# Weight tiles split into two parts by casting and accumulating DMAs from DRAM, with no raw copy in SBUF

## The chip, the cores and the metric

The kernel runs on one core of one Trainium2 chip. The metric is device time in microseconds (us) of one execution. Lower is better. The core has five engines with instruction queues of their own, each worked off in order: PE (matrix products; PEld is its weight load), DVE (VectorE), ACT (ScalarE), POOL (GpSimd) and SP (SyncE). SP and POOL both issue DMAs here: SP's go through the hardware queue q1, POOL's through the software queue q0. Both are carried out by the same 16 DMA engines.

## The reference

One decoder block over 512 tokens (plus 16 meta tokens put in front) of width 1024, all in float32:

```
h = concat(meta, x)                                   # (528, 1024)
proj = rmsnorm(h, g_mix) @ w_in                       # z 1024 | xbc 1536 | dt 16 | u 1024 columns
y_ssd = ssd(silu(conv(xbc)), dt, z)                   # Mamba-2 heads: 16 heads, state 128
y_s5  = glu(gelu(s5(u)) @ w_glu + b_glu)              # 64 groups, state 64; w_glu (1024, 2048)
h = h + concat(y_ssd, y_s5) @ w_out                   # w_out (2048, 1024)
h = h + square(relu(rmsnorm(h, g_mlp) @ w_up)) @ w_down   # w_up (1024, 4096), w_down (4096, 1024)
out = rmsnorm(h, g_final)[16:]
```

## The kernel before

A float32 product is made from three products of operands in the rounded format `fp32r`: each operand is split into a high part `hi` (the value rounded) and a low part `lo` (the rest, rounded), and PE adds hi x hi, hi x lo and lo x hi into one PSUM bank (`mm_cols` for weights on the stationary side, `rows_product` for weights on the moving side). So every weight has to be loaded and split before PE can use it.

Weights come in tiles of 128 partitions x 1024 values (512 KB). There are 92 of them that go through the functions which the change touches, in this order of use: 8 column tiles of `w_in` for u (first projection), 8 for z, 12 for xbc, 16 of `w_glu`, 16 row tiles of `w_out`, 32 column tiles of `w_up`. A column tile is 8 x 128 pieces of 128 values (512 bytes) in DRAM, a row tile 2 x 128 pieces of 512 values (2 KB). The weights of `w_down` (32 tiles, called `quad` and `quads`) are loaded and split by other functions.

`load_weight` has SP load a tile into `raw` (two buffers). `split_weight` then makes `whi` and `wlo` (three buffers each) in one of two ways. With `lo_engine` V (45 tiles: one of u, 12 of `w_out`, 32 of `w_up`) ACT casts `raw` to `whi` and DVE subtracts. Otherwise (47 tiles: 7 of u, z, xbc, `w_glu` and 4 of `w_out`) ACT writes -raw, rounded, to `wlo`, a DMA issued by POOL adds `raw` to it from SBUF, and ACT casts `raw` to `whi`.

The stages overlap. While PE works on z and xbc, it, DVE and ACT also work off the blocks of the S5 scan (`s5_block`, with tiles `px`, `py`, `pb`, `pk`). While it works on the GLU (`pv`, `pg`), the chunks of the SSD run, which need large broadcasts from DRAM (`ab`, `erep`) and a masking step on POOL (the affine select). In the MLP four quarters follow each other: 8 tiles of `w_up` (`pm`), then a down product (`acc`, `acct`) in which two tiles of the next quarter are already used. At the start POOL also computes the powers of the first norm (`rstd`).

The order of the instructions on each engine is set by a scheduler that plays the program through with its own times before it is built. `tc.high_priority(offset=3000)` moves the loads and the splits forward in it as far as their buffers allow; within an engine's queue nothing overtakes on the chip. PSUM has three banks (`mm`) for the products with column tiles.

Of the kernel before, what the change touches and what calls it, by code (L numbers as in the profile page):

```python
# [18 lines left out]
P = 128  # L19
# [5 lines left out]
KD = DM // P  # L25
# [4 lines left out]
O_U = 2576  # L30
# [8 lines left out]
AHEAD = 3000  # L39
# [14 lines left out]
def hybrid_block_kernel(ctx, tc, x, meta_tokens, g_mix, w_in, conv_w, conv_b, dt_bias, a_log, d_ssd,  # L54
                        g_ssd, lam_re, lam_im, log_step, b_re, b_im, c_re, c_im, d_s5, w_glu, b_glu,
                        g_s5, w_out, g_mlp, w_up, w_down, g_final, out, dbg=None):
    nc = tc.nc
    V, A, G, T = nc.vector, nc.scalar, nc.gpsimd, nc.tensor
    dma = nc.sync.dma_start
# [8 lines left out]
    wp = ctx.enter_context(tc.tile_pool(name="wp", bufs=2))  # L68
# [30 lines left out]

    def load_weight(src, a, b, ahead=AHEAD):
        with (tc.high_priority(offset=ahead) if ahead else nullcontext()):
            raw = wp.tile([P, a, b], F32, tag="raw", name="raw", bufs=2)
            dma(out=raw, in_=src)
        return raw

    def split_weight(raw, lo_engine=None, ahead=AHEAD, room=None):
        with (tc.high_priority(offset=ahead) if ahead else nullcontext()):
            if room is None:  # L110
                hi = wp.tile(list(raw.shape), F32R, tag="hi", name="whi", bufs=3)
                lo = wp.tile(list(raw.shape), F32R, tag="lo", name="wlo", bufs=3)
            else:
                hi, lo = room("whi", list(raw.shape)), room("wlo", list(raw.shape))
            if lo_engine is V:
                A.copy(hi, raw)  # L116
                V.tensor_tensor(out=lo, in0=raw, in1=hi.bitcast(F32), op=ALU.subtract)  # L117
            else:

                A.mul(lo, raw, -1.0)  # L120
                G.dma_start(out=lo.bitcast(F32), in_=raw, accum_op=ALU.add)  # L121
                A.copy(hi, raw)  # L122
        return hi, lo

    def load_cols(w, c0, n=P, ahead=AHEAD):
        return load_weight(w[:, c0:c0 + n].rearrange("(k p) c -> p k c", p=P), KD, n, ahead)

    def w_cols(w, c0, n=P, lo_engine=None):
        return split_weight(load_cols(w, c0, n), lo_engine)

    def w_rows(w, k0, c0, lo_engine=None, room=None):
        return split_weight(load_weight(w[k0 * P:(k0 + 2) * P, c0:c0 + 512].rearrange("(k p) c -> p k c", p=P),
                                        2, 512), lo_engine, room=room)

    def mm_cols(ps_out, w, x, m, tok):
        steps = [(k, a, b) for k in range(KD) for a, b in ((0, 0), (0, 1), (1, 0))]
# [55 lines left out]
    first_raw = {}  # L192
# [49 lines left out]
    uw, uts = {}, {}  # L242

    def u_split(f):
        raw = first_raw[f] if f in first_raw else load_cols(w_in[0], O_U + f * P)
        uw[f] = split_weight(raw, V if f == 2 else G, 0 if f < 3 else AHEAD)
        uts[f] = s5.tile([P, TS5, NC5], F32, tag="ut", name="ut", bufs=2)

    def u_half(f, i):
# [180 lines left out]
    for part, (x0, x1, op) in enumerate(((bRt, bIt, ALU.subtract), (bIt, bRt, ALU.add))):  # L430
# [3 lines left out]
                        in1=tb2.rearrange("p (b j) h -> p b j h", b=8), op=op)  # L434
# [236 lines left out]
    for f in range(8):  # L671
        w = w_cols(w_in[0], f * P)
# [15 lines left out]
    for f in order:  # L688
        w = w_cols(w_in[0], O_XBC + f * P)
# [4 lines left out]
    for n, f in enumerate(order):  # L694
        raw = xbc_tile(f)
# [27 lines left out]
    for ch in range(NCH):  # L723
        n = NM if ch == 0 else P
# [14 lines left out]
        if ch > 0:  # L739
            lt = slice((ch - 1) * P, ch * P)  # L740
            erep = sd.tile([P, KD, P], F32, tag="erep", name="erep", bufs=1)
            for q in range(2):
                dma2(out=erep[64 * q:64 * q + 64],
                     in_=eD.rearrange("(r q) l -> q r l", q=2)[q, :, lt].partition_broadcast(64))
# [14 lines left out]
            for h in range(2):  # L759
# [8 lines left out]
                for r in range(4):  # L768
# [6 lines left out]
                                op=ALU.mult)  # L775
# [38 lines left out]
    token_rstd(s1, pq1[:, 0:4])  # L814


    def rows_product(lhs, w, rows0, n_slab, c0, lo_engine, finish, room=None):
        acc = [None if room else bank("acc") for _ in range(4)]

        def mms(sl, wt, t):  # L820
            for k in range(2):
                for n, (a, b) in enumerate(((0, 0), (1, 0), (0, 1))):
                    T.matmul(acc[t], lhsT=lhs[2 * sl + k][a][:, t * P:(t + 1) * P], rhs=wt[b][:, k],  # L823
                             start=(sl == 0 and k == 0 and n == 0), stop=(sl == n_slab - 1 and k == 1 and n == 2))


        tail = 1 if room is None else n_slab
        for sl in range(n_slab - tail):
            wt = w_rows(w, rows0 + 2 * sl, c0, lo_engine)
            for t in range(4):  # L830
                mms(sl, wt, t)
        last = [(sl, w_rows(w, rows0 + 2 * sl, c0, lo_engine, room if sl else None))
                for sl in range(n_slab - tail, n_slab)]
# [36 lines left out]
    y5hi = slot("y5hi", [P, KD, SEQ], F32R)  # L870
    y5lo = slot("y5lo", [P, KD, SEQ], F32R)
# [31 lines left out]
    s2 = mid.tile([P, 4], F32, tag="s5_s", name="s5_s", bufs=1)  # L903
    token_rstd(s2, pq2[:, 0:4])
    for c0 in (0, 512):
        rows_product([(y5hi[:, k], y5lo[:, k]) for k in range(KD)], w_out[0], 8, 4, c0, V, add_scaled(s2))
    yhi = slot2("yhi", [P, KD, SEQ], F32R)
    ylo = slot2("ylo", [P, KD, SEQ], F32R)
    for f in range(8):
        A.activation(out=yhi[:, f], in_=xc[:, f, NM:L], func=AF.Copy, scale=col("gssd", f))  # L910
        V.scalar_tensor_tensor(out=ylo[:, f], in0=xc[:, f, NM:L], scalar=col("gssd", f),
                               in1=yhi[:, f].bitcast(F32), op0=ALU.mult, op1=ALU.subtract)
# [17 lines left out]
        transpose_split(xs[:, t], P, hhi, hlo, t * P)  # L930

    ylist = [(yhi[:, k], ylo[:, k]) for k in range(KD)]
    rows_product(ylist, w_out[0], 0, 4, 0, G, mix_first)
    spare = iter(("S", "xdt", "xde", "erep", "ab", "ab"))

    def spare_room(name, shape):
        tag = next(spare)
        return sd.tile(shape, F32R, tag=tag, name=name, bufs=2 if tag == "ab" else 1)

    rows_product(ylist, w_out[0], 0, 4, 512, V, mix_second, room=spare_room)  # L940


    sd_ctx.__exit__(None, None, None)
# [211 lines left out]
```

## Time and profile before

| | |
|---|---|
| three runs | 854.35, 854.48, 850.58 us |
| median | 854.35 us |
| profiled execution, its own time | 849.42 us |
| its span in the profile | 847.7 us |
| mean granted TensorE clock | 0.976 |
| instructions in the span | 11641 |
| bytes on q1 (SP's DMAs) | 90.89 MB, 37.1% of the 16 engines' span |
| bytes on q0 (POOL's DMAs) | 24.64 MB, 15.6% |

The profile is one execution. Its page gives busy times of the engines, the span in 40 slices with a digit for the busy tenths, the DMA queues, and a chain of waits: the work that ended last, followed back from the end. Other views list groups of instructions (how many, busy time, mean of one in ns, then the idle time of the engine before them and what ended it), a tile's instructions (min/median/max in ns, then first and last start in us), and a stretch of the span. A matmul's recorded time overlaps with that of the next one, so PE's pace is read from the distance of starts, or from a piece of the chain and its count.

### The profile page before, as it was taken

To read this page: it belongs to the slowest core of one execution; us is meant where nothing else is said; L and a number is where in the kernel's file an instruction comes from. 1 tells how busy PE (TensorE), PEld (TensorE's weight loads), DVE (VectorE), ACT (ScalarE), POOL (GpSimd) and SP (SyncE) were. 2 spreads that over 40 slices of the span, in tenths; PEclk is the share of its full clock that TensorE was granted. 3 is DMA by queue.
4 is the path that set the end of the run, shared out by engine and by line. 5 is a ranking of instruction groups with operands and counts; after the bars stand their busy time and mean duration, and the time that the engine had idled before them with its cause. 6 is when DMAs were issued, how large, how long until landed. Compare 5 with 4: busy or idle time off the path is not lost.

```text
span 847.7 us, 11641 instructions
## 1 busy us (share of the span) xinstructions
PE 793.3 (94%) x4351; PEld 668.9 (79%) x4351; DVE 585.5 (69%) x961; ACT 453.8 (54%) x714; POOL 66.9 (8%) x115
## 2 busy tenths in 40 slices
PE   5998699999996789988999999999999999999996
PEld 4898588999994667776888888888888888888874
DVE  6873688899973585561631567688848884887396
ACT  7575678798664457474313344354334524443264
POOL 5101010101010122111001010000000000000001
PEclk9999899999998899999999999999999999999999
DMA  9887666677657568778426636434133422331002
GB/s 221 188 201 188 149 154 146 168 156 171 153 143 169 162 136 186 164 208 212 144 98 149 176 97 224 125 99 150 51 98 100 150 71 83 118 127 49 1 2 99
DMA packets 144865, 116.28 MB, mean 137 GB/s; under 512 B 22092, under 2 KB 122616, under 8 KB 144808
## 3 DMA queue, kind: packets, MB, share of 16 engines
q1 hardware_dynamic: 138040, 90.89, 37.1%
q0 software_dynamic: 6768, 24.64, 15.6%
q8 instruction: 34, 0.56, 0.3%
q14 instruction: 23, 0.19, 0.1%
HBM read 83.93 MB, written 6.95 MB: 107 GB/s over the span
## 4 chain that ended last, share of the span: by engine, by line
PE 66%; DMA 17%; issue 4%; ACT 4%; SPq 4%; DVE 3%; POOL 0%; POOLq 0%; ACTq 0%; DVEq 0%
PE pm L138 21%; PE acc L1066 15%; PE acc L823 8%; DMA wlo<-raw 6%; PE pxb L138 4%; PE pz L138 4%; DMA raw<-in_w_in_dram 4%; DMA ab<-aD 3%; PE acct L823 3%; PE acct L1066 3%; DMA yf<-Yd 2%; PE pg L138 1%; PE px L561 1%; PE pv L138 1%; ACT wlo L120 1%
## 5 line engine op out<-in xcount | busy, mean ns | idle before, releaser
L117 DVE TENSOR_TENSOR wlo<-raw,whi 128x1024 fp32r<-128x1024 f32 x45 | 55.0, 1222 | 78.4 <-ACT whi L116 78.3
L138 PE MATMUL pm<-hhi,wlo 128*128 128x512 f32 (+1 forms) x272 | 103.6, 381 | 0.0
L138 PE MATMUL pm<-hlo,whi 128*128 128x512 f32 (+1 forms) x272 | 103.5, 381 | 0.0
L138 PE MATMUL pm<-hhi,whi 128*128 128x512 f32 (+1 forms) x272 | 103.0, 381 | 0.0
L116 ACT CAST whi<-raw 128x1024 fp32r<-128x1024 f32 x45 | 47.2, 1049 | 101.5 <-PE pm L138 60.3
L122 ACT CAST whi<-raw 128x1024 fp32r<-128x1024 f32 x47 | 49.0, 1043 | 57.8 <-PE acc L823 15.3
L1066 PE MATMUL acc<-bh,al 128*128 128x512 f32 x192 | 75.1, 391 | 0.1
L1066 PE MATMUL acc<-bl,ah 128*128 128x512 f32 x192 | 75.0, 391 | 0.0
L1066 PE MATMUL acc<-bh,ah 128*128 128x512 f32 x192 | 69.5, 392 | 1.4 <-ACT ah L970 1.4
L121 POOL DMA_DIRECT2D wlo<-raw x47 | 40.2, 856 | 313.4 <-ACT wlo L120 148.0
L970 ACT CAST bh<-quad 128x1024 fp32r<-128x1024 f32 x32 | 33.7, 1053 | 49.4 <-PE acc L1066 42.3
L138 PEld LDWEIGHTS pm<-hlo,whi 128*128 128x128 f32 x272 | 51.1, 188 | 10.9
L138 PEld LDWEIGHTS pm<-hhi,whi 128*128 128x128 f32 x272 | 51.0, 188 | 10.8
L138 PEld LDWEIGHTS pm<-hhi,wlo 128*128 128x128 f32 x272 | 51.0, 188 | 10.4
L138 PE MATMUL pxb<-xhi,whi 128*128 128x264 f32 x192 | 56.3, 293 | 0.0
L138 PE MATMUL pxb<-xlo,whi 128*128 128x264 f32 x192 | 56.2, 293 | 0.0
L138 PE MATMUL pxb<-xhi,wlo 128*128 128x264 f32 x192 | 56.0, 292 | 0.0
L120 ACT ACTIVATE wlo<-raw 128x1024 fp32r<-128x1024 f32 x47 | 49.6, 1054 | 8.6 <-DMA raw<-in_w_glu_dram 8.1
L965 DVE TENSOR_TENSOR bl<-quad,bh 128x1024 fp32r<-128x1024 f32 x32 | 39.1, 1221 | 18.6 <-ACT bh L970 18.6
L970 ACT CAST bh<-quads 128x1024 fp32r<-128x1024 f32 x24 | 25.2, 1049 | 40.8 <-PE acc L1066 26.7
L1066 PEld LDWEIGHTS acc<-bh,ah 128*128 128x128 f32 x192 | 35.9, 188 | 9.7 <-ACT ah L970 2.1
L1066 PEld LDWEIGHTS acc<-bh,al 128*128 128x128 f32 x192 | 36.0, 188 | 8.3 <-DVE al L965 0.5
(374 smaller groups left out, 2062.6 us busy)
## 6 DMA issues: line engine op xcount, KB each, us to landing
wlo<-raw POOLq DMA_DIRECT2D x47, 512.0 KB, 5.1
raw<-in_w_up_dram SPq DMA_DIRECT2D x32, 512.0 KB, 4.0
raw<-in_w_in_dram SPq DMA_DIRECT2D x28, 512.0 KB, 4.0
raw<-in_w_glu_dram SPq DMA_DIRECT2D x16, 512.0 KB, 4.4
raw<-in_w_out_dram SPq DMA_DIRECT2D x16, 512.0 KB, 3.2
quad<-in_w_down_dram SPq DMA_DIRECT2D x16, 512.0 KB
quads<-in_w_down_dram SPq DMA_DIRECT2D x16, 512.0 KB, 6.0
ab<-aD SPq DMA_DIRECT2D x8, 512.0 KB, 6.5
```

The lines of the kernel that those rows point to most:

```text
L116: A.copy(hi, raw)
L117: V.tensor_tensor(out=lo, in0=raw, in1=hi.bitcast(F32), op=ALU.subtract)
L120: A.mul(lo, raw, -1.0)
L121: G.dma_start(out=lo.bitcast(F32), in_=raw, accum_op=ALU.add)
L122: A.copy(hi, raw)
L138: T.matmul(ps_out, lhsT=w[a][:, k, 0:m], rhs=x[b][:, k, tok], start=(n == 0), stop=(n == len(steps) - 1))
L561: T.matmul(p[:, j * NC5:(j + 1) * NC5], lhsT=w[:, 2 * hf + j], rhs=ub[:, 2 * hf + j])
L823: T.matmul(acc[t], lhsT=lhs[2 * sl + k][a][:, t * P:(t + 1) * P], rhs=wt[b][:, k], start=(sl == 0 and k == 0 and n == 0), stop=(sl == n_sl ...
L965: V.tensor_tensor(out=out, in0=a, in1=b, op=ALU.subtract)
L970: A.copy(hi, src)
L1066: T.matmul(banks[bk][s], lhsT=as_[g][x][:, j, s * P:(s + 1) * P], rhs=bs[g][y][:, j], start=(first and g == 0 and j == 0 and i == 0), stop ...
```

## The change

All 92 tiles are treated alike. `whi` is written by a DMA from POOL that reads float32 from DRAM and writes `fp32r`, which rounds. ACT writes -whi to `wlo`. A second DMA from POOL reads the same weights from DRAM again and adds them to `wlo`. The tile `raw`, ACT's casts, DVE's subtractions and the choice of `lo_engine` go away. `whi` and `wlo` have four buffers each where they had three. The diff, without the callers that only drop `lo_engine`:

```diff
-    def load_weight(src, a, b, ahead=AHEAD):
+    def load_hi(src, a, b, ahead=AHEAD, hi=None):
         with (tc.high_priority(offset=ahead) if ahead else nullcontext()):
-            raw = wp.tile([P, a, b], F32, tag="raw", name="raw", bufs=2)
-            dma(out=raw, in_=src)
-        return raw
-
-    def split_weight(raw, lo_engine=None, ahead=AHEAD, room=None):
+            if hi is None:
+                hi = wp.tile([P, a, b], F32R, tag="hi", name="whi", bufs=4)
+            G.dma_start(out=hi, in_=src)
+        return hi, src
+
+    def split_weight(part, ahead=AHEAD, lo=None):
+        hi, src = part
         with (tc.high_priority(offset=ahead) if ahead else nullcontext()):
-            if room is None:
-                hi = wp.tile(list(raw.shape), F32R, tag="hi", name="whi", bufs=3)
-                lo = wp.tile(list(raw.shape), F32R, tag="lo", name="wlo", bufs=3)
-            else:
-                hi, lo = room("whi", list(raw.shape)), room("wlo", list(raw.shape))
-            if lo_engine is V:
-                A.copy(hi, raw)
-                V.tensor_tensor(out=lo, in0=raw, in1=hi.bitcast(F32), op=ALU.subtract)
-            else:
-                A.mul(lo, raw, -1.0)
-                G.dma_start(out=lo.bitcast(F32), in_=raw, accum_op=ALU.add)
-                A.copy(hi, raw)
+            if lo is None:
+                lo = wp.tile(list(hi.shape), F32R, tag="lo", name="wlo", bufs=4)
+            A.mul(lo, hi.bitcast(F32), -1.0)
+            G.dma_start(out=lo, in_=src, accum_op=ALU.add)
         return hi, lo
...
-    def w_rows(w, k0, c0, lo_engine=None, room=None):
-        return split_weight(load_weight(w[k0 * P:(k0 + 2) * P, c0:c0 + 512].rearrange("(k p) c -> p k c", p=P),
-                                        2, 512), lo_engine, room=room)
+    def w_rows(w, k0, c0, room=None):
+        src = w[k0 * P:(k0 + 2) * P, c0:c0 + 512].rearrange("(k p) c -> p k c", p=P)
+        if room is None:
+            return split_weight(load_hi(src, 2, 512))
+        hi, lo = (room(nm, [P, 2, 512]) for nm in ("whi", "wlo"))
+        return split_weight(load_hi(src, 2, 512, hi=hi), lo=lo)
```

What this does to the queues, at three places (a name's number tells tiles apart; the `whi` and the `wlo` of one tile have neighbouring numbers).

POOL in the middle of the xbc stage, before:

```order
L121 DMA wlo_2598<-raw_2595 128x1024
L121 DMA wlo_2657<-raw_2654 128x1024
L121 DMA wlo_2716<-raw_2713 128x1024
L121 DMA wlo_2775<-raw_2772 128x1024
L121 DMA wlo_2834<-raw_2831 128x1024
L121 DMA wlo_2893<-raw_2890 128x1024
```

POOL at the same place now:

```order
L107 DMA whi_2554<-in_w_in_dram 128x8x128
L117 DMA wlo_2556<-in_w_in_dram 128x8x128
L107 DMA whi_2611<-in_w_in_dram 128x8x128
L117 DMA wlo_2613<-in_w_in_dram 128x8x128
L107 DMA whi_2668<-in_w_in_dram 128x8x128
L117 DMA wlo_2670<-in_w_in_dram 128x8x128
L107 DMA whi_2725<-in_w_in_dram 128x8x128
L117 DMA wlo_2727<-in_w_in_dram 128x8x128
```

The loads, which stood in SP's queue, now stand between the accumulates, each behind the accumulate of the tile before it.

POOL in the output product (`w_out`), now; before there were accumulates for four of its tiles only:

```order
L107 DMA whi_4314<-in_w_out_dram 128x2x512
L117 DMA wlo_4316<-in_w_out_dram 128x2x512
L107 DMA whi_4343<-in_w_out_dram 128x2x512
L117 DMA wlo_4345<-in_w_out_dram 128x2x512
L107 DMA whi_4404<-in_w_out_dram 128x2x512
L107 DMA whi_4433<-in_w_out_dram 128x2x512
L117 DMA wlo_4406<-in_w_out_dram 128x2x512
L117 DMA wlo_4435<-in_w_out_dram 128x2x512
```

Here single tiles (load, accumulate) and pairs (two loads, two accumulates) take turns; in the MLP nearly all are pairs, in z and xbc nearly all single.

ACT in the xbc stage, now (`pxb` is the product in PSUM, copied to `bcr` in two halves per tile):

```order
L691 COPY bcr_2266<-pxb_2331 128x264
L116 ACTIVATE wlo_2499<-whi_2497 128x1024
L544 ACTIVATE co_1708<-ta_1704,ones_80 128x528
L691 COPY bcr_2266<-pxb_2357 128x264
L699 ACTIVATE bcr_2266<-bcr_2266 128x528
```

The negation of `whi_2497` stands ahead of the second half's copy of a tile that is used three tiles earlier. Before, a cast and a negation of the same `raw` stood at such a place; now there is the negation alone, and it waits for a load that POOL issues.

POOL at the start, now:

```order
L107 DMA whi_99<-in_w_in_dram 128x8x128
L90 AFFINE_SELECT tri_77<-tri_77 128x128
L107 DMA whi_102<-in_w_in_dram 128x8x128
L107 DMA whi_606<-in_w_in_dram 128x8x128
L107 DMA whi_665<-in_w_in_dram 128x8x128
L345 MEMSET mtab_470 128x1 x10
L149 TENSOR_TENSOR rstd_143<-ssq_140,mhalf_82 16x1
```

Four loads come ahead of the first `rstd`, which no DMA of POOL preceded before.

More of the change, by code (lines that the diff above doesn't have):

```diff
@@ L123, in split_weight @@
+    def split_weight(part, ahead=AHEAD, lo=None):
+        hi, src = part
+        with (tc.high_priority(offset=ahead) if ahead else nullcontext()):
+            if lo is None:
+                lo = wp.tile(list(hi.shape), F32R, tag="lo", name="wlo", bufs=4)
+            A.mul(lo, hi.bitcast(F32), -1.0)
+            G.dma_start(out=lo, in_=src, accum_op=ALU.add)
         return hi, lo
     def load_cols(w, c0, n=P, ahead=AHEAD):
-        return load_weight(w[:, c0:c0 + n].rearrange("(k p) c -> p k c", p=P), KD, n, ahead)
@@ L128, in w_cols @@
-    def w_cols(w, c0, n=P, lo_engine=None):
-        return split_weight(load_cols(w, c0, n), lo_engine)
-    def w_rows(w, k0, c0, lo_engine=None, room=None):
-        return split_weight(load_weight(w[k0 * P:(k0 + 2) * P, c0:c0 + 512].rearrange("(k p) c -> p k c", p=P),
-                                        2, 512), lo_engine, room=room)
+        return load_hi(w[:, c0:c0 + n].rearrange("(k p) c -> p k c", p=P), KD, n, ahead)
+    def w_cols(w, c0, n=P):
+        return split_weight(load_cols(w, c0, n))
@@ L244, in u_split @@
     def u_split(f):
-        raw = first_raw[f] if f in first_raw else load_cols(w_in[0], O_U + f * P)
-        uw[f] = split_weight(raw, V if f == 2 else G, 0 if f < 3 else AHEAD)
+        part = first_raw[f] if f in first_raw else load_cols(w_in[0], O_U + f * P)
+        uw[f] = split_weight(part, 0 if f < 3 else AHEAD)
         uts[f] = s5.tile([P, TS5, NC5], F32, tag="ut", name="ut", bufs=2)
@@ L814, in hybrid_block_kernel, with rows_product @@
     token_rstd(s1, pq1[:, 0:4])
-    def rows_product(lhs, w, rows0, n_slab, c0, lo_engine, finish, room=None):
+    def rows_product(lhs, w, rows0, n_slab, c0, finish, room=None):
         acc = [None if room else bank("acc") for _ in range(4)]
@@ L828, in rows_product @@
         for sl in range(n_slab - tail):
-            wt = w_rows(w, rows0 + 2 * sl, c0, lo_engine)
+            wt = w_rows(w, rows0 + 2 * sl, c0)
             for t in range(4):
                 mms(sl, wt, t)
-        last = [(sl, w_rows(w, rows0 + 2 * sl, c0, lo_engine, room if sl else None))
+        last = [(sl, w_rows(w, rows0 + 2 * sl, c0, room if sl else None))
                 for sl in range(n_slab - tail, n_slab)]
@@ L905, in hybrid_block_kernel @@
     for c0 in (0, 512):
-        rows_product([(y5hi[:, k], y5lo[:, k]) for k in range(KD)], w_out[0], 8, 4, c0, V, add_scaled(s2))
+        rows_product([(y5hi[:, k], y5lo[:, k]) for k in range(KD)], w_out[0], 8, 4, c0, add_scaled(s2))
     yhi = slot2("yhi", [P, KD, SEQ], F32R)
@@ L932, in hybrid_block_kernel @@
     ylist = [(yhi[:, k], ylo[:, k]) for k in range(KD)]
-    rows_product(ylist, w_out[0], 0, 4, 0, G, mix_first)
+    rows_product(ylist, w_out[0], 0, 4, 0, mix_first)
     spare = iter(("S", "xdt", "xde", "erep", "ab", "ab"))
@@ L938, in spare_room @@
         return sd.tile(shape, F32R, tag=tag, name=name, bufs=2 if tag == "ab" else 1)
-    rows_product(ylist, w_out[0], 0, 4, 512, V, mix_second, room=spare_room)
+    rows_product(ylist, w_out[0], 0, 4, 512, mix_second, room=spare_room)
     sd_ctx.__exit__(None, None, None)
@@ L952, in up_tile @@
     def up_tile(q, f, r):
-        w = w_cols(w_up[0], (8 * q + f) * P, lo_engine=V)
+        w = w_cols(w_up[0], (8 * q + f) * P)
         pm = bank("pm")
@@ L1111, in hybrid_block_kernel @@
         if q == 0:
-            pre = [(bank("pm"), w_cols(w_up[0], f * P, lo_engine=V)) for f in range(2)]
+            pre = [(bank("pm"), w_cols(w_up[0], f * P)) for f in range(2)]
             for tok in (slice(0, SEQ // 2), slice(SEQ // 2, SEQ)):
```

## The prediction

> **What bounds the kernel now.** I read the page's busy times, slices and chain first, then the span cut into stages, then the DMA queues in stretches where one kind of transfer runs nearly alone.
>
> ```profile
> PE 793.3 (94%) x4351; PEld 668.9 (79%) x4351; DVE 585.5 (69%) x961; ACT 453.8 (54%) x714; POOL 66.9 (8%) x115
> DMA  9887666677657568778426636434133422331002
> PE 66%; DMA 17%; issue 4%; ACT 4%; SPq 4%; DVE 3%; POOL 0%; POOLq 0%; ACTq 0%; DVEq 0%
> ```
>
> TensorE is busy 94% of the span, so little can be won; the DMA engines are far from full on average, but not in the first half. The stages (columns: length, then busy time of PE, PEld, DVE, ACT, POOL with counts, clock, DMA share, GB/s):
>
> ```profile
> 0.00:42.00 42.00, 29.84 (x204) 27.79 (x205) 32.80 (x87) 27.46 (x54) 13.68 (x53) 0.92 0.90 205
> 95.00:158.00 63.00, 57.59 (x360) 48.58 (x360) 50.40 (x105) 47.63 (x74) 5.94 (x7) 0.95 0.63 146
> 158.00:260.00 102.00, 99.88 (x861) 97.75 (x860) 90.54 (x159) 80.83 (x124) 9.32 (x11) 0.98 0.68 158
> 260.00:300.00 40.00, 28.11 (x133) 20.77 (x134) 20.91 (x33) 16.79 (x40) 5.59 (x5) 0.83 0.61 162
> 380.00:412.00 32.00, 29.14 (x126) 22.92 (x125) 7.11 (x11) 12.98 (x18) 3.64 (x4) 1.00 0.83 213
> 412.00:505.00 93.00, 93.00 (x419) 75.80 (x418) 44.67 (x62) 33.49 (x47) 6.17 (x8) 1.00 0.43 122
> 600.00:850.00 250.00, 238.67 (x1033) 193.27 (x1032) 181.39 (x229) 104.32 (x144) 3.07 (x4) 0.99 0.26 80
> ```
>
> PE has holes at the head and around 260 to 300, hardly any between 158 and 260 or in the MLP. The pace at which PE consumes weight tiles, from the first and last starts of each stage's matmuls and from long pieces of the chain:
>
> ```profile
> L138 PEld LDWEIGHTS pu<-xhi,whi x128: 186/188/331, 15.4 to 78.0; 128*128 128x128 f32 x128
> L138 PEld LDWEIGHTS pz<-xhi,whi x64: 186/188/330, 80.8 to 153.1; 128*128 128x128 f32 x64
> L138 PEld LDWEIGHTS pxb<-xhi,whi x192: 186/188/329, 153.8 to 258.2; 128*128 128x128 f32 x192
> L138 PEld LDWEIGHTS pv<-yghi,whi x64: 187/188/330, 267.3 to 405.7; 128*128 128x128 f32 x64
> 427.10 53.26 PE acc L823 x228
> 764.67 35.23 PE pm L138 x151
> ```
>
> The first projection uses a tile every (80.8 - 15.4)/8 = 8.2 us, z every (153.8 - 80.8)/8 = 9.1, xbc every (258.2 - 153.8)/12 = 8.7, the GLU stage about (412 - 267)/16 = 9.1. The output product takes 53.26/228 = 0.234 us a matmul, 24 to a tile: 5.6 us; the up product 35.23/151 x 24 = 5.6 us.
>
> **What is removed.** The work on a weight tile today:
>
> ```profile
> L121 POOL DMA_DIRECT2D wlo<-raw x47 | 40.2, 856 | 313.4 <-ACT wlo L120 148.0 <-ACT xcr L693 62.0 <-ACT ut L252 58.8
> L120 ACT ACTIVATE wlo<-raw 128x1024 fp32r<-128x1024 f32 x47 | 49.6, 1054 | 8.6 <-DMA raw<-in_w_glu_dram 8.1
> L122 ACT CAST whi<-raw 128x1024 fp32r<-128x1024 f32 x47 | 49.0, 1043 | 57.8 <-PE acc L823 15.3
> L116 ACT CAST whi<-raw 128x1024 fp32r<-128x1024 f32 x45 | 47.2, 1049 | 101.5 <-PE pm L138 60.3
> L117 DVE TENSOR_TENSOR wlo<-raw,whi 128x1024 fp32r<-128x1024 f32 x45 | 55.0, 1222 | 78.4 <-ACT whi L116 78.3
> L105 SPq DMA_DIRECT2D raw<-in_w_up_dram x32: 367/368/368, 479.4 to 774.2; - x32
> ```
>
> ACT loses 92 casts (49.0 + 47.2 = 96.2 us) and gains 45 negations (45 x 1.054 = 47.4): 49 us less. DVE loses 55.0 us. Neither engine ends a stage that PE fills, and the waits of L117 and L116 are idle time of DVE and ACT, not of PE; I cost the removal at 0. Also gone are 92 plain loads of about 0.37 us each, 34 us of SP's queue, which is no bound.
>
> **What is added.** POOL issues 184 DMAs where it issued 47. A column tile comes in 8 x 128 = 1024 pieces of 512 B, where the accumulating DMA of before had 128 rows of 4 KB. No row shows such an issue. The nearest rows:
>
> ```profile
> L121 POOL DMA_DIRECT2D wlo<-raw x47: 838/854/1023, 10.2 to 466.9; - x47
> DMA to landing us min/median/max: 4.5/5.1/10.3
> 0.31 0.10 POOL L1141 MEMSET const-float32-0.0<- 128x1 f32 x1 [0.31 <-issue]
> ```
>
> Lower end: 0.85 us, if the issue doesn't depend on the pieces. Upper end: all but the 0.10 us of the smallest POOL instruction grows with them, 0.75 x 8 + 0.1 = 6.1 us. I take 1.5 us, nearer the row, since 128 pieces are little work beside the start of an instruction; for the output weights (256 pieces) 1.0 us. The Trainium skill, "DMA: Bandwidth & Descriptors", section "Anatomy of one DMA — SWDGE (gpsimd) path", calls descriptor generation small and says that many can be emitted before the incremental cost shows; by that it would be 0.85 and the sum below some 15 us smaller. No run here shows it yet.
>
> The transfers: three stretches, 598 to 634 us (six `w_up` tiles nearly alone), 425 to 480 (output weights, four accumulates) and 158 to 230 (columns: packets, MB, share of 16 engines):
>
> ```profile
> q1 hardware_dynamic: 6240, 3.15, 30.7%
> ...
> raw<-in_w_up_dram SPq DMA_DIRECT2D x6, 512.0 KB, 4.1
> q1 hardware_dynamic: 2678, 5.16, 28.0%
> q0 software_dynamic: 576, 2.10, 20.0%
> ...
> wlo<-raw POOLq DMA_DIRECT2D x4, 512.0 KB, 5.0
> q1 hardware_dynamic: 15779, 7.36, 38.4%
> ```
>
> A copied column tile takes 0.307 x 36/6 = 1.84 us of all 16 engines; a copied tile in 2 KB pieces 0.28 x 55/(5.16/0.524) = 1.56; an accumulate with 4 KB rows 0.20 x 55/4 = 2.75, or 1.76 times the copy. For an accumulate in 512 B pieces the lower end is 2.75; the upper end is eight times the packets at the same time each, 22 us. I take 1.84 x 1.76 = 3.25, as 512 B copies cost only 1.18 times the 2 KB ones. The casting load I take as a copy, 1.84 (if it works like an accumulate, 3.25). From the last byte to the semaphore: 5.1 - 0.85 - 2.75 = 1.5 us. Other traffic in 158 to 230: 0.384 x 72 - 8 x 1.84 = 12.9 of 72 us, 18%.
>
> **The new wait.** In the z and xbc stages POOL's order is strictly `whi` of a tile, its `wlo`, the next `whi`. The `wlo` waits for the negation, which waits for `whi` to land, and the next load stands behind it on POOL. On the software queue that load's data also stand behind the accumulate. One tile per turn of this loop: issue 1.5, transfers (3.25 + 1.84)/0.82 = 6.2, landing 1.5, ACT's queue 1.0 (an estimate, about one ACT operation), negation 1.05: 11.3 us. ACT's order holds the negation ahead of PSUM evacuations, so a late load also stalls those, and PE behind them. Four buffers hide latency, not a loop slower than PE.
>
> Rows for the terms (a wait of POOL; the DMA queue and the loads in 260 to 412 us; POOL's first `pow`; two starts of the chain):
>
> ```profile
> POOL ab L751 <- DMA ab<-aD: 47.7, 7, 15.8
> q1 hardware_dynamic: 28903, 19.81, 47.7%
> ...
> raw<-in_w_glu_dram SPq DMA_DIRECT2D x12, 512.0 KB, 4.4
> 4.85 0.54 POOL L151 TENSOR_TENSOR rstd<-ssq,mhalf 16x1 f32<-16x1 f32 x1 [1.94 <-DVE ssq L149]
> 598.82 34.67 PE pm L138 x150
> 681.47 35.23 PE pm L138 x151
> ```
>
> Terms:
> - z, 8 x (11.3 - 9.1) = 18; xbc, 12 x (11.3 - 8.7) = 31; less one tile of lead, 9: **+40**.
> - GLU: four tiles strict, the rest mostly in groups of two or three. Other traffic is (0.477 x 152 - 12 x 1.84 - 3 output tiles x 1.56)/152 = 0.3, so the strict loop takes 1.5 + 5.1/0.7 + 3.55 = 12.3, 3.2 over the pace, or 13 for four; PE's hole at 260 to 300 (11.9 us) hides most of that. POOL also waits 47.7 us with its eight affine selects, and now both loads of a tile stand behind them where only the accumulate did: I put a fifth of it on PE, **+10**.
>
> - Output product: singles take 1.0 + 2.75 + 1.56 + 1.5 + 0.3 + 1.05 = 8.2 against 5.6, pairs 9.7 for two. Six singles cost 15, three pairs give 4, lead covers 5: **+6**.
> - Head: four loads go out ahead of the first `pow` on POOL, done near 1.9 + 4 x 1.5 = 7.9 us where it ran at 4.85; the DMA share is 0.90 there already: **+3**.
>
> - MLP: pairs take 1.5 + 3.25 + 3.7 + 1.5 + 0.3 + 1.05 = 11.3 for two, 5.6 each, PE's own pace with four tiles in hand; the cover is the down product, during which no more than two tiles are used. **0**; if the accumulate takes 2 us more, four tiles of each quarter are late by 1 to 2 us, about 20 in all.
>
> Sum: 40 + 10 + 6 + 3 = 59 us. The profiled execution took 849.4 us (span 847.7), 5 us under the median of 854.35 of the three runs shown. 849.4 + 59 = **908 us**.
>
> **Rivals.**
> *Hidden, or faster.* The loop closes within PE's pace when the issue is 0.85, the accumulate 2.75 and ACT's wait 0.3: 0.85 + 4.59/0.82 + 2.85 = 9.3 us, which one tile of lead covers over 20 tiles. It decides at 8.7 to 9.1 us. Then the time stays at 849 to 854. If lighter ACT and DVE queues also close small holes (2.9 us in 380 to 412, 5.4 in 95 to 158), it is 841. For it: ACT is 79% and DVE 89% busy in 158 to 260. Against: PE is 98% busy there. Chance 0.11 for no change, 0.09 for faster. The Trainium skill, same page, section "Issuing engines are not separate DMA queues", says that moving a transfer to another issuer only changes issue time, since all share 16 engines; by that alone the time would be this one. It leaves out the queue order on POOL, which is my reason; no run here shows which holds.
>
> *POOL is the bound.* At 6.1 us an issue the loop is 2 x 6.1 + 3.55 = 15.8: z 54, xbc 85, GLU 16 x 6.7 = 107, first projection 8 x 7.6 = 61, output 15, head 20; each MLP quarter (598.8 to 681.5) needs 16 x 6.1 = 98 of 83 us, 4 x 15 = 60: +402, 1250 us. It decides from about 4 us, where the two issues outlast the transfers. Against: an issue of 128 pieces takes 0.85. The same would follow if issues are held up by VectorE. For that the Trainium skill, "SBUF — State Buffer", section "SBUF: two separate sides", has a rule: a VectorE operation in a two-port mode locks GpSimd out while it writes descriptors. The longest of 47 issues took 1.02 us with DVE busy 69%, so the trace shows no such delay. Chance 0.11.
>
> *The small-piece accumulate is slow.* At 6 to 8 us the loop is 1.5 + 8.8/0.82 + 3.55 = 15 to 17: some +220 over the same stages, and 40 in the MLP: 1000 to 1110 us. Chance 0.10.
>
> **Chances.** Forecast (slower by 20 to 100 us) 0.59, the two worse cases 0.21, no change 0.11, faster 0.09. The forecast's own range is 870 to 950. For 8 in 10 the low end is 850, which leaves out the faster case; the high end 1020, which leaves out most of the two worse ones. 0.5% is about what three runs of this kernel can tell: faster 0.09, same 0.11, slower 0.80.
>
> **What would show it.** POOL's DMA issues at 1 to 2 us, 184 of them; SP's queue without L105; 97 MB on q0, and accumulates of 3 to 4 us; waits of POOL's `wlo` for ACT and of ACT's `wlo` for the DMA of `whi`; z and xbc longer by 35 to 45 us with PE idle inside; MLP unchanged within 5 us. Wrong if an issue stays at 0.85 and the loop under 9 us, if issues reach 4 us, or if the MLP grows.

## The result, and the profile after

The changed kernel takes 949.09 us (median of four runs, 942.47 to 950.20) against 852.47 us for the kernel before on the same chip: 1.114 times, 95% interval 1.109 to 1.118. The forecast was 908 us, with a range of 870 to 950: the median lies 1 us inside its end. The profiled execution took 948.63 us (span 946.9) against 849.42, so 99 us are to be explained where the sum had 59. Ratios and intervals leave out the few runs that were more than 1.5% above the fastest of their kernel; medians count every run.

The page of the changed kernel: busy times, DMA share in 40 slices, POOL's queue, and the chain by engine.

```profile
PE 819.3 (87%) x4351; PEld 681.4 (72%) x4351; DVE 536.5 (57%) x916; ACT 411.4 (43%) x666; POOL 246.2 (26%) x252
DMA  9999887778876939999976795999659659956702
q0 software_dynamic: 166784, 96.48, 69.1%
PE 35%; issue 29%; DMA 20%; POOL 10%; ACT 3%; DVE 2%; SPq 1%; POOLq 0%; ACTq 0%
```

PE does the same 4351 matmuls, but is busy 87% of a longer span. Its part of the chain falls from 66% to 35%, and POOL, which had none, has 10%. Another 29% is "issue", time for which the profile names nothing that was waited for. DVE and ACT lost 49 and 42 us of work, near the 55 and 49 of the prediction. POOL's busy time grows from 67 to 246 us, far from its limit.

PE's weight loads by stage (first and last start) give the pace, as before:

```profile
L136 PEld LDWEIGHTS pu<-xhi,whi x128: 187/188/333, 20.9 to 88.1; 128*128 128x128 f32 x128
L136 PEld LDWEIGHTS pz<-xhi,whi x64: 186/188/334, 90.8 to 174.1; 128*128 128x128 f32 x64
L136 PEld LDWEIGHTS pxb<-xhi,whi x192: 187/188/338, 179.3 to 300.2; 128*128 128x128 f32 x192
L136 PEld LDWEIGHTS pv<-yghi,whi x64: 186/188/334, 318.1 to 476.9; 128*128 128x128 f32 x64
```

Cut at the first matmul of each stage (the GLU from its first `pv` to its last `pg`), the time went here, in us; "forecast" is the term in the prediction's sum:

| stage | before | after | difference | forecast |
|---|---|---|---|---|
| start to the first z matmul | 80.8 | 90.8 | +10.0 | +3 |
| z | 73.3 | 88.7 | +15.4 | |
| xbc | 104.4 | 121.1 | +16.7 | |
| end of xbc to first GLU matmul | 8.8 | 17.5 | +8.7 | z to here: +40 |
| GLU | 144.7 | 164.6 | +19.9 | +10 |
| to the first up matmul (output product) | 92.0 | 105.6 | +13.6 | +6 |
| MLP, to the end | 343.7 | 358.6 | +14.9 | 0 |

The turn on POOL that the forecast was built on stands in the timeline of POOL in the xbc stage (start, duration, what, idle before and what ended it):

```profile
199.15 1.53 POOL L117 DMA_DIRECT2D wlo<-in_w_in_dram  x1 [5.04 <-ACT wlo L116]
...
231.64 1.53 POOL L117 DMA_DIRECT2D wlo<-in_w_in_dram  x1 [7.50 <-ACT wlo L116]
232.54 1.55 POOL L107 DMA_DIRECT2D whi<-in_w_in_dram  x1
241.87 1.53 POOL L117 DMA_DIRECT2D wlo<-in_w_in_dram  x1 [7.78 <-ACT wlo L116]
...
273.74 1.54 POOL L117 DMA_DIRECT2D wlo<-in_w_in_dram  x1 [8.60 <-ACT lag L527]
```

From 199.15 to 273.74 POOL issues seven more accumulates: 10.66 us a tile. In three of these seven turns the load first waits 0.7 to 2.1 us for PE to free a buffer; in the others nothing stands between it and the accumulate before. One such turn, from the chain of that stretch:

```profile
231.64 0.62 POOL wlo L117
...
232.54 7.87 DMA whi<-in_w_in_dram
...
240.43 1.06 ACT wlo L116
```

The load goes out right behind the accumulate of the tile before, lands 7.87 us later, ACT negates for 1.06 us, and only then can the next accumulate go, with the next load behind it. Waits of the whole span (total, times, longest) say the same:

```profile
POOL wlo L117 <- ACT wlo L116: 307.6, 59, 9.5
POOL whi L107 <- PE pm L136: 118.4, 17, 22.8
DVE r L960 <- ACT rl L959: 109.6, 21, 10.6
ACT wlo L116 <- DMA whi<-in_w_up_dram: 105.4, 22, 10.2
ACT wlo L116 <- DMA whi<-in_w_in_dram: 86.6, 22, 9.4
```

How a late load reaches PE is seen in PE's own waits in the xbc stage, 180 to 300 us after the change:

```profile
PE pb L513 <- ACT yb L589: 8.4, 3, 4.6
PE px L559 <- issue: 3.1, 1, 3.1
PE px L559 <- ACT bti L515: 2.9, 1, 2.9
PE pk L522 <- ACT btr L515: 2.0, 1, 2.0
```

Before the change the longest one there, 154 to 258 us, was:

```profile
PE py L585 <- DMA Tp<-Kd: 1.9, 1, 1.9
```

PE waits 16.4 us in all where it waited 2.3, and the stage is 16.7 us longer. None of it is put down to a weight tile. 13.3 us are waits for ACT's copies of the S5 blocks (`yb`, `btr`, `bti`), and these stand in ACT's queue behind a negation that waits for its load, as here:

```profile
240.43 1.06 ACT L116 ACTIVATE wlo<-whi 128x1024 fp32r<-128x1024 f32 x1 [3.07 <-DMA whi<-in_w_in_dram]
241.39 0.57 ACT L515 COPY btr<-pb 128x512 f32<-128x512 f32 x1
```

In the output product and in the MLP PE does wait for the tiles themselves: 8.8 and 5.2 us for `wlo`.

### The profile page after: what moved, and what is told of

Same layout as the page of the kernel before. It is cut to its first block, busy times and chain, and to the rows that moved or that the text cites. A ratio compares the mean times of both kernels' runs of the same rounds, so it can differ in the third digit from the quotient of the medians.

```text
span 946.9 us, 11594 instructions
## 1 busy us (share of the span) xinstructions
PE 819.3 (87%) x4351; PEld 681.4 (72%) x4351; DVE 536.5 (57%) x916; ACT 411.4 (43%) x666; POOL 246.2 (26%) x252
## 3 DMA queue, kind: packets, MB, share of 16 engines
q0 software_dynamic: 166784, 96.48, 69.1%
## 4 chain that ended last, share of the span: by engine, by line
PE 35%; issue 29%; DMA 20%; POOL 10%; ACT 3%; DVE 2%; SPq 1%; POOLq 0%; ACTq 0%
PE acc L1064 11%; PE pm L136 9%; DMA whi<-in_w_in_dram 7%; POOL wlo L117 5%; POOL whi L107 4%; DMA whi<-in_w_up_dram 3%; DMA ab<-aD 3%; PE acct L821 3%; DMA wlo<-in_w_glu_dram 2%; PE pv L136 2%; PE pg L136 2%; PE acct L1064 1%; DMA whi<-in_w_glu_dram 1%; PE acc L821 1%; PE pxb L136 1%
## 5 line engine op out<-in xcount | busy, mean ns | idle before, releaser
L116 ACT ACTIVATE wlo<-whi 128x1024 fp32r<-128x1024 f32 x92 | 97.3, 1060 | 311.2 <-DMA whi<-in_w_up_dram 105.4
L117 POOL DMA_DIRECT2D wlo<-in_w_in_dram x28 | 45.0, 1681 | 162.5 <-ACT wlo L116 111.2
L960 DVE SCALAR_TENSOR_TENSOR r<-pm,rl 128x512 f32<-128x512 f32 x32 | 22.1, 690 | 110.0 <-ACT rl L959 109.6
L117 POOL DMA_DIRECT2D wlo<-in_w_up_dram x32 | 49.9, 1575 | 118.3 <-ACT wlo L116 82.6
L107 POOL DMA_DIRECT2D whi<-in_w_up_dram x32 | 38.1, 1212 | 123.8 <-PE pm L136 118.4
L136 PE MATMUL pu<-xhi,whi 128*128 128x264 f32 x128 | 38.4, 301 | 4.9 <-ACT ut L250 4.4
L117 POOL DMA_DIRECT2D wlo<-in_w_glu_dram x16 | 24.8, 1573 | 68.1 <-ACT wlo L116 46.9
```

What stands on the lines that cost most here:

```text
L107: G.dma_start(out=hi, in_=src)
L116: A.mul(lo, hi.bitcast(F32), -1.0)
L117: G.dma_start(out=lo, in_=src, accum_op=ALU.add)
L136: T.matmul(ps_out, lhsT=w[a][:, k, 0:m], rhs=x[b][:, k, tok], start=(n == 0), stop=(n == len(steps) - 1))
L960: V.scalar_tensor_tensor(out=r, in0=pm, scalar=0.0, in1=rl, op0=ALU.max, op1=ALU.mult)
```

## The experiments

Three theories, with the letters that some expectations use. **A, POOL's order**: the accumulate of a tile waits for its own load, and the next load stands behind it, so load, negation and accumulate never overlap from tile to tile. **B, traffic**: the weights are read twice from DRAM, and the DMA engines or their bytes are the limit. **C, pieces**: it is the 1024 pieces of 512 bytes in each transfer, by their issue and their transfer. Stages are cut as in the table above, from one profiled execution each.

### order: the next load ahead of the accumulate

```diff
+    def next_weight():            # sources of z, xbc, GLU, w_out, w_up stand in a queue
+        while queue and len(ready) < 2:
+            part = load_hi(*queue.pop(0)); ready.append((part, load_ins[-1]))
+        part, _ = ready.pop(0)
+        return split_weight(part, after=ready[0][1] if ready else None)
...
-            G.dma_start(out=lo, in_=src, accum_op=ALU.add)
+            with (tc.issue_after(after.ins) if after is not None else nullcontext()):
+                G.dma_start(out=lo, in_=src, accum_op=ALU.add)
```

> The same DMAs and buffers as the changed kernel; only POOL's order differs from z on: the load of tile k+1 stands ahead of the accumulate of tile k, so no load waits for a negation. Theory A (the load that stands behind the accumulate on POOL and on the software queue sets the pace, about 10.7 us a tile): xbc back to about 9 us a tile, the total to 900 to 920 us. Rival B (the 16 engines' added work, a second read and casting, sets the pace in any order): 940 to 955 us.

Measured: 871.93 us, 1.027 times before (1.022 to 1.032), better than A had it. It is 24 us above the kernel before, measured beside it, where the changed kernel was 97 above: some 73 us are gone, with the same bytes, pieces, issues and operations. POOL in the xbc stage, and the landings of loads and accumulates:

```profile
194.58 0.89 POOL L107 DMA_DIRECT2D whi<-in_w_in_dram  x1 [6.63 <-PE pxb L148]
195.46 1.59 POOL L129 DMA_DIRECT2D wlo<-in_w_in_dram  x1
...
whi<-in_w_in_dram POOLq DMA_DIRECT2D x28, 512.0 KB, 5.1
wlo<-in_w_in_dram POOLq DMA_DIRECT2D x28, 512.0 KB, 7.3
```

POOL no longer waits for ACT between the two, but for PE to free a buffer: PE sets the pace again. A load lands after 5.1 us where it took 8.1 in the changed kernel, now that it goes out ahead of the accumulate. PE's waits in xbc shrink from 16.4 to 2.2 us, and xbc takes 99.9 us, less than before the change. A is shown to carry most of the loss, and B falls as its main cause.

### noacc: no accumulates

```diff
-            G.dma_start(out=lo, in_=src, accum_op=ALU.add)
```

> Leaves out the accumulating DMA: wlo is only the negated whi, so the low parts are wrong. The 92 casting loads stay on POOL. Theory A: nothing is left for a load to stand behind, 855 to 875 us. Rival B: half of the added transfers stay, about 900 us. Rival C (the casting loads by POOL are themselves slow, 1024 pieces each): over 910 us.

Measured: 824.05 us, 0.970 times before (0.965 to 0.975), faster than all three theories had it and faster than before; casting loads are not slow in themselves, so C falls in that form. With casting loads, lighter queues of ACT and DVE and no accumulate at all there would be 24 us to win (z 67.9, xbc 97.4, GLU 131.2 us); each kernel measured against the one before, the accumulates cost about 121 us in the changed order and 48 us in the mended one. POOL's queue without them:

```profile
q0 software_dynamic: 83392, 48.24, 31.5%
```

The MLP is worth a look:

```profile
ACT wlo L116 <- DMA whi<-in_w_up_dram: 87.2, 30, 7.4
DVE r L959 <- ACT rl L958: 78.3, 22, 4.9
```

ACT still waits 87.2 us for the loads in front of its `relu` (105.4 in the changed kernel), and yet the MLP takes 343.0 us as before. That wait alone is covered; it costs time only together with the accumulates.

### rows: the same transfers in 4 KB rows

```diff
-        return load_hi(w[:, c0:c0 + n].rearrange("(k p) c -> p k c", p=P), KD, n, ahead)
+        k = next(turn_rows) % 8
+        return load_hi(w[k * P:(k + 1) * P, 0:KD * n].rearrange("p (k c) -> p k c", k=KD), KD, n, ahead)
```

Each tile is read as 128 rows of 4 KB, as many bytes (the row tiles of `w_out` likewise).

> Reads other weights: every tile as 128 rows of 4 KB in DRAM instead of 1024 pieces of 512 bytes (the values are wrong, bytes, order and buffers are the same). Rival C (pieces): the issue falls from 1.5 to about 0.86 us, the accumulate to 2.75 us, the total to 860 to 880 us. Theory A: the loop only loses those 0.7 + 0.3 + 0.4 us a tile, 915 to 930 us. Rival B: 940 us or more.

Measured: 907.40 us, 1.069 times before (1.064 to 1.075), between the ranges of C and A. Issues of the accumulates, of this kernel and then of the changed one:

```profile
L117 POOL DMA_DIRECT2D wlo<-in_w_in_dram x28: 837/844/1620, 8.8 to 251.5; - x28
```

```profile
L117 POOL DMA_DIRECT2D wlo<-in_w_in_dram x28: 1522/1534/3544, 12.9 to 273.7; - x28
```

1024 pieces instead of 128 add 0.69 us to an issue. C is worth about 37 of the 97 us, by 0.69 us for each issue and by slower transfers, which this run doesn't tell apart; with it gone the same order still costs 6.9%. None of the gain is in the MLP, which takes 363.9 us here and 358.6 in the changed kernel. The Trainium skill, "DMA: Bandwidth & Descriptors", section "Anatomy of one DMA — SWDGE (gpsimd) path", calls descriptor generation small; the rows agree on the size and show that it is not nothing on a path where two issues follow each other.

### dvelo: no accumulates, the low part by DVE from a raw tile

```diff
+            raw = wp.tile([P, a, b], F32, tag="raw", name="raw", bufs=2)
+            dma(out=raw, in_=src)                        # SP
...
-            A.mul(lo, hi.bitcast(F32), -1.0)
-            G.dma_start(out=lo, in_=src, accum_op=ALU.add)
+            V.tensor_tensor(out=lo, in0=src, in1=hi.bitcast(F32), op=ALU.subtract)
```

The weights are read twice here too (139.9 MB in all, as in the changed kernel), with three buffers each for `whi` and `wlo`.

> Same bytes from DRAM as the changed kernel, but the second read is a plain load by SP into raw, and DVE subtracts (three buffers of whi and wlo, two of raw, as before). POOL keeps the 92 casting loads. Theory A: no accumulate and no loop, 855 to 880 us, more only where DVE is full in xbc. Rival B (two reads from DRAM, 97 MB): over 920 us.

Measured: 872.56 us, 1.028 times before (1.023 to 1.034). z takes 66.0 and xbc 93.1 us, both shorter than before. But then PE waits 45.8 us for the GLU where it waited 8.8. The stretch from 160 to 260 us (columns as in the prediction), and POOL's longest wait:

```profile
160.00:260.00 100.00, 89.29 (x746) 86.27 (x745) 95.18 (x159) 51.30 (x92) 9.62 (x11) 0.94 0.70 151
...
POOL ab L750 <- DMA yf<-Yd: 51.9, 1, 51.9
```

DVE is busy 95% there. The S5 scan, whose results (`yf`) come late, shares its queue with 27 added subtractions of u, z and xbc (33 us), the likeliest cause. PE lost twice in one wait what it had won in z and xbc. For B the run says more: with all the bytes and pieces of the changed kernel the first z matmul comes at 82.0 us (80.8 before), and z and xbc are faster than before.

### issuer: the kernel before, its plain loads issued by POOL

```diff
-            dma(out=raw, in_=src)
+            G.dma_start(out=raw, in_=src)
```

> The kernel before, with one thing changed: the 92 plain loads of raw tiles are issued by POOL instead of SP. Bytes, pieces, casts and accumulates (out of SBUF) stay as before. Queue theory: in the stages with accumulates a turn is issue 0.9 + 0.85, transfers (2.75 + 1.84)/0.82 = 5.6, landing 1.5, ACT's wait 1.0, negation 1.05: 10.9 us against 9.1 and 8.7, so z +14, xbc +26, less a tile of lead 9, GLU about +8, output product and MLP 0 to +3 (no accumulates there but four): 880 to 895 us. Rival, the issuer doesn't matter and what costs is the second read from DRAM in small pieces: 846 to 856 us.

Measured: 869.14 us, 1.023 times before (1.018 to 1.028). Slower, but by less than the queue theory had it and not where it was expected: z 74.9 and xbc 101.7 us are as before; the start takes 7.7 us more and the GLU 12.9. POOL in xbc:

```profile
198.75 0.91 POOL L105 DMA_DIRECT2D raw<-in_w_in_dram  x1 [4.85 <-DMA wlo<-raw]
199.64 0.90 POOL L121 DMA_DIRECT2D wlo<-raw  x1
206.61 0.91 POOL L105 DMA_DIRECT2D raw<-in_w_in_dram  x1 [6.07 <-DMA wlo<-raw]
209.24 0.85 POOL L121 DMA_DIRECT2D wlo<-raw  x1 [1.73 <-ACT xcr L693]
```

The load here is that of two tiles on: it waits for the accumulate that frees its raw buffer, and the accumulate behind it belongs to the tile before, which landed earlier. One tile of lead in the order is enough here. The changed kernel had four buffers but no lead in the order. The Trainium skill, "DMA: Bandwidth & Descriptors", section "Issuing engines are not separate DMA queues", has the choice of issuer save only the short time of issue: z and xbc agree (+1.6 and -2.7 us), the whole does not (+18 us of 851). In the GLU the loads now share a queue with POOL's affine selects, which wait for broadcasts, and PE waits 14.1 us there for `wlo` where it waited 3.3; that the selects are the cause was not tested apart.

### head, order_head, order_head2: the start

`head` is the changed kernel with the first accumulates behind the powers of the norm on POOL; `order_head` does that in `order` and puts the tiles of the first projection into its queue; `order_head2` also puts the first negations behind the last square on ACT.

```diff
     prepare(0)
-    u_split(0)
     prepare(1)
     prepare(2)
-    u_half(0, 0)
     prepare(3)
+    u_split(0)
+    u_half(0, 0)
     u_split(1)
...
+            with tc.issue_after(last_pow[-1].ins):
                 G.dma_start(out=lo, in_=src, accum_op=ALU.add)
...
+            with (nullcontext() if ahead else tc.issue_after(last_sq[-1].ins)):   # order_head2
                 A.mul(lo, hi.bitcast(F32), -1.0)
```

> The changed kernel, with the first accumulates put on POOL behind all five powers of the first norm (and the token tiles prepared ahead of the first weight tile's split). Queue theory: the head grew by about 10 us because two powers stand behind an accumulate that waits for a landing of 9.8 us; with them ahead, 6 to 10 us come back: 937 to 945 us. Rival, traffic: the head is late because the DMA engines are full there (share over 1 in the first 28 us), and the order of POOL changes nothing: 946 to 952 us.

> The kernel 'order' (872 us), with the tiles of the first projection put into the same order (load of the next tile ahead of the accumulate) and the first accumulates behind the powers of the norm. Queue theory: the head and the first projection, 10.6 us above the kernel before, fall to 0 to 4 above it: 860 to 867 us. Rival, traffic in the head: 870 to 875 us.

> The kernel 'order_head' (870.9 us; first matmul of z at 91.9 us), with the first negations on ScalarE put behind the last square of the first norm; nothing else is moved. Theory, ScalarE's order: two to three squares stand on ScalarE behind a negation that waits 4.8 us for the first weight tile's landing, so the token tiles come late to TensorE; with the squares ahead the first matmul of z comes 4 to 8 us earlier, at 84 to 88 us, and the whole takes 862 to 867 us. Rival, traffic: the token tiles and weights land late in the head, and z begins at 90 to 93 us as before, 868 to 874 us.

Measured: `head` 957.55 us (1.128 times before, 1.120 to 1.137), no gain but a little slower than the changed kernel; `order_head` 870.87 (1.025, 1.017 to 1.032), as `order`; `order_head2` 867.59 (1.019, 1.015 to 1.024), not told from `order_head` by the intervals. The first z matmul came at 97.4, 91.9 and 91.2 us. ACT in `head`:

```profile
11.77 1.06 ACT L116 ACTIVATE wlo<-whi 128x1024 fp32r<-128x1024 f32 x1 [4.86 <-DMA whi<-in_w_in_dram]
12.73 1.04 ACT L147 ACTIVATE scr<-xt 128x1024 f32<-128x1024 f32 x1
```

A square of the norm stands behind the first negation, which waits 4.86 us for its load: POOL's order was not all that held the powers. With that mended too, PE starts on u at 17.5 us instead of 25, and loses it again:

```profile
L150 PEld LDWEIGHTS pu<-xhi,whi x128: 187/188/333, 17.5 to 88.9; 128*128 128x128 f32 x128
...
PE pc L456 <- DMA scr<-in_c_re_dram: 9.8, 1, 9.8
scr<-in_c_re_dram SPq DMA_DIRECT2D x2, 256.0 KB, 12.7
```

The rows of `c_re` land 12.7 us after their issue, during three accumulates, where they took 4.1 in the changed kernel. Whichever queue is put right, another transfer of the start is late. Without accumulates (`noacc`) the first z matmul comes at 76.8 us, before the change at 80.8. That suggests traffic, but other runs speak against bytes as the cause: `dvelo` reads all weights twice and is there at 82.0 us, while `issuer`, with the bytes of before, needs 88.5 and `rows` 89.8, with a DMA share of 0.79 and 0.78 in the first 80 us (0.85 before). The late starts (`issuer`, `rows`, the changed kernel, the three here, and `cast` and `cast_free` below) have weight loads and accumulates together in POOL's queue from the start; the early ones don't. What in that costs the 10 us stays open.

### cast and cast_free: only the high part by a casting load

The kernel before, with `raw` loads by SP and low parts as they were, and `whi` by a casting load instead of ACT's cast. In `cast` the next tile's load is put ahead of the accumulate as in `order`; in `cast_free` it follows it.

```diff
             dma(out=raw, in_=src)
-        return raw
+            hi = hi if hi is not None else wp.tile([P, a, b], F32R, tag="hi", name="whi", bufs=3)
+            G.dma_start(out=hi, in_=src)
+        return raw, hi
...
-                A.copy(hi, raw)
```

> The kernel before, with only the rounded part changed: whi by a casting load from DRAM on POOL (next tile's load ahead of the accumulate), raw tiles and low parts as before (accumulate from the raw tile in SBUF, or VectorE). ScalarE loses all 92 casts and gains nothing. Queue theory: nothing on POOL waits for a load that POOL has issued, so the loop is open; the lighter ScalarE gives z -5, xbc -8, GLU 0 to -3, the MLP 0 to +3: 833 to 848 us. Rival, traffic: raw 1.84 + whi 1.84 + accumulate 2.75 = 6.4 us of all DMA engines a tile, with 18% other traffic 0.92 of the pace in xbc: the loads come late and it is slower, 865 to 900 us.

> The kernel 'cast' (948.4 us) with the next tile's casting load no longer put ahead of the accumulate: on POOL the order is load of a tile, its accumulate, the next load, as in the changed kernel, but the accumulate waits for a raw tile that SP has loaded. Bytes and pieces are those of 'cast' (164.5 MB). Theory, the buffer: in 'cast' the accumulate of a tile stood behind a load that waits until TensorE is done with the tile two ahead, which left one tile for a landing of 7.5 us; now it is two tiles, and the lighter ScalarE shows: 833 to 855 us. Rival, traffic: with 164.5 MB the loads come late whatever the order: 925 to 950 us.

Measured: `cast` 948.36 us (1.116, 1.108 to 1.124), `cast_free` 915.42 (1.074, 1.067 to 1.080). My theory missed both by far, and neither rival's range holds them. POOL in the z stage of `cast`, then in that of `cast_free`, with two stretches (columns as in the prediction), a median landing and a wait of PE:

```profile
139.64 0.91 POOL L107 DMA_DIRECT2D whi<-in_w_in_dram  x1 [17.39 <-PE pz L150]
140.53 0.90 POOL L131 DMA_DIRECT2D wlo<-raw  x1
```

```profile
160.06 0.92 POOL L107 DMA_DIRECT2D whi<-in_w_in_dram  x1 [6.77 <-PE pz L138]
161.38 0.85 POOL L119 DMA_DIRECT2D wlo<-raw  x1 [0.40 <-ACT wlo L118]
...
0.00:80.00 80.00, 56.74 (x406) 53.94 (x406) 53.88 (x150) 39.15 (x79) 23.79 (x63) 0.89 1.09 224
160.00:260.00 100.00, 86.68 (x681) 81.70 (x681) 80.42 (x145) 61.23 (x101) 17.68 (x20) 0.93 0.91 189
wlo<-raw POOLq DMA_DIRECT2D x47, 512.0 KB, 7.3
...
PE py L586 <- DMA Tp<-Kd: 17.8, 3, 11.1
```

In `cast` an accumulate stands behind a load that waits for PE to free one of three buffers, so it goes out with one tile left to land in; the order that gained some 73 us with the four buffers of `order` costs about 31 here with three. `cast_free` mends that, but 164.5 MB now go through the DMA engines, accumulates from SBUF land after 7.3 us where they took 5.1 before, and z still takes 92.5 us. The last line is PE's longest wait in z: not for weights, but for `Tp`, small tiles of the S5 scan that go through DRAM (`Kd`) on SP's queue. That fits traffic that delays small transfers, so B at 164.5 MB; but no run takes bytes away with the order kept, and it is not shown.

### late_glu: a part of the change where it has room

The kernel before, with casting loads and DVE subtractions for ten of the sixteen GLU tiles.

```diff
-        wv = w_cols(w_glu[0], f * P)
+        wv = w_cols_cast(w_glu[0], f * P) if f >= 3 else w_cols(w_glu[0], f * P)
```

(`wg` likewise; `w_cols_cast` loads `raw` by SP and `whi` by a casting DMA, and subtracts on DVE.)

> The kernel before, with one thing taken over from the change for ten of the sixteen GLU tiles (f from 3 on): whi by a casting load from DRAM on POOL, the low part by VectorE from the raw tile, no accumulate. In that stretch of the kernel before VectorE is busy 21 of 52 us and TensorE 46.1 of 52, and the chain runs through accumulates. Theory: nothing on POOL waits for a load that POOL has issued, VectorE has room for 10 x 1.22 us, ScalarE loses ten casts and ten negations (21 us): the hole of 5.9 us closes in part, 3 to 6 us faster than before, 843 to 848 us. Rival, POOL's queue: loads of whi stand behind the affine selects there, as the raw tiles do in 'issuer' (its GLU stage took 13 us more): 3 to 10 us slower, 853 to 860 us.

Measured: 846.73 us against 852.31, 0.994 times (0.991 to 0.997): apart from `noacc`, which leaves the accumulates out, the only kernel here that beats the one before, by 0.3 to 0.9%. The last part of the GLU, which before had PE busy 46.12 and DVE 20.97 of 52 us:

```profile
360.00:412.00 52.00, 50.38 (x242) 40.68 (x243) 32.49 (x52) 18.09 (x28) 5.46 (x6) 0.97 0.81 206
```

PE's hole is nearly closed, DVE has taken the work, and the bytes are those of before (116.3 MB), since each second read takes the place of an accumulate. The GLU takes 141.9 us where it took 144.7. The whole profiled execution (850.68 us, one of the longer of twelve) is no shorter than that of before, so the gain in the whole rests on the medians.

## Why the prediction was right, and where it was short

**The mechanism was right; that the z and xbc term came out to 1 us is partly luck.** The turn was put at 11.3 us and measured at 10.66 (9.7 to 11.2 between single issues). Issue, transfers and landing were put at 9.2; in the turn shown above they take 8.8, 0.90 from the accumulate's start to the load's and 7.87 from there to the landing. ACT's wait and the negation were put at 2.05 and take about 1.1 and a little, since ACT mostly stood waiting for the load. `order` shows that POOL's order is the cause.

Errors cancelled inside this, in two places. First, the transfers were put too small. Read as the prediction read them (share of the 16 engines times span), a casting load takes 0.315 x 817.7/92 = 2.8 us in `noacc`, where 1.84 was put, and an accumulate (0.691 x 946.9 - 0.315 x 817.7)/92 = 4.3 us, an estimate, where 3.25 was put. With these the prediction's own sum for a turn would have been 1.5 + 7.1/0.82 + 3.55 = 13.7 us, 3 more than measured: the parts overlap more than the sum allowed. Second, with the measured turn its arithmetic gives 8 x 1.56 + 12 x 1.96 - 9 = 27 us, not 40. z and xbc lost 32.1, less than the 35 to 45 it named, and the other 8.7 are the wait between xbc and the GLU, which had no term. The way to PE in xbc was the one that the prediction names last, ACT's order, and not a missing tile.

**By its own list of signs the prediction was wrong on the MLP**: it was to stay within 5 us and grew by 14.9. The accumulates, at an estimated 4.3 us, lie a little over the 3 to 4 it named. The issues, 96.48 MB on q0, and the waits of `wlo` for ACT and of ACT for `whi` came as named.

**The rivals.** "Hidden, or faster" falls: at 10.66 us the loop doesn't close within 8.7 to 9.1. "POOL is the bound" falls: issues stay at 1.5 us, and `order` runs within 2.7% of before with all 184. The longest issue of an accumulate was 3.5 us, in the first projection, the median of the 28 on `w_in` 1.53, so no lock-out by VectorE of the size feared is seen. "The small-piece accumulate is slow" falls as stated: landing takes 5.8 to 8.0 us with the queue in front of it, the transfer an estimated 4.3 and not 6 to 8, and `rows` gives back 37 us, not 220.

**The steps that were mis-sized** are the four small terms, together 19 us forecast and 58 measured:

- *MLP, 0, measured +14.9.* Pairs were put at 11.3 us, equal to PE's own pace. The timeline of POOL has two pairs from 609.60 to 634.64, 12.5 us each:

```profile
609.60 1.56 POOL L117 DMA_DIRECT2D wlo<-in_w_up_dram  x1 [6.73 <-ACT wlo L116]
...
634.64 1.56 POOL L117 DMA_DIRECT2D wlo<-in_w_up_dram  x1 [5.40 <-ACT wlo L116]
```

  1.3 us over PE's 11.2 for 16 pairs are 21 us, and the down product covers some of them. A term that is a difference of two equal numbers was set to 0 with no room above it; the text's own "about 20" for a slower accumulate was nearer. Transfers that are too slow aren't enough as the cause: in `rows` they take 0.478 x 904.3/184 = 2.3 us on average (3.6 in the changed kernel), and the MLP loses 20.2 us all the same. In `order` it loses 5.6, so most of it is the order again.
- *GLU, +10, measured +19.9.* A fifth of POOL's waits with the affine selects was put on PE. `issuer` loses 12.9 us in that stage with loads alone moved onto POOL, and `order` 8.1 with the strict turn gone; both parts were taken too small, and the runs don't split them exactly. PE waits 11.9 us in this stage for weight tiles, where it waited 3.3 before.
- *Output product, +6, measured +13.6.* Single tiles were put at 8.2 us a turn. They take 8.6 to 9.0, and 10.3 to 11.0 where two loads go out together; an issue takes 1.2 us, not 1.0. `order`, which removes the turn, takes 92.1 us, as before.
- *Head, +3, measured +10.* The forecast looked only at POOL's powers. The first wait is ACT's, for the first load; three kernels that mended the queues there did not get the time back, and the cause stays open.

With the 40.8 of z, xbc and the wait behind them these make the 99.2 us measured. The range held by 1 us only: the forecast's own ended at 950, and the wide one at 1020.

## What to carry to other kernels

When a load and an instruction that waits for it go through one queue, look at the order of the queue and not at its busy time: POOL was busy 26% and its order cost some 73 us. Follow the wait to the engine that is the bound: here it went by a third engine's queue (ACT's), in which other work stood behind the waiting instruction. Put the next load ahead of the waiting instruction, but only with a buffer that is free without the tile in use; in `cast`, with three buffers, the same order cost about 31 us. And where a stage runs close to its limit, a term that comes out as "just enough" is not 0: give it the price of one step of its uncertainty, times the number of turns.

## What was not expected of the hardware

- A casting load is cheap: 512 KB in 1024 pieces are issued in 0.88 us and land after 4.6 to 4.8 us in `noacc`, hardly later than a plain load from SP before the change (4.0 to 4.4). In the changed kernel, where many loads stand behind an accumulate in POOL's queue, they land after 7.6 to 8.1.
- Leaving the accumulates out made the kernel 3% faster than before the change, though PE was busy 94% of it. The removals were costed at 0 in the prediction because no stage ends on ACT or DVE; together with the accumulates' landings they were worth 24 us (30 between the profiled executions), nearly half of it in the GLU (144.7 to 131.2).
- PE's granted clock is lower in the kernels in which PE waits more: 0.976 before (PE busy 94%), 0.949 after (87%), 0.987 without accumulates (96%). PE's busy time for the same matmuls is 26 us longer after the change (819.3 against 793.3), so part of the 99 us may be the clock. Which way round the cause runs was not tested.
